# Up projection as a seven-product Strassen scheme, with separate up and down phases, in a two-layer streaming encoder

## The chip, the cores and the metric

The kernel runs on one core of a Trainium2 chip. The metric is the device time of one execution in microseconds (us), as the median of several runs. The engines are called PE (matrix products; PEld is its weight load), DVE (elementwise work on vectors), ACT (functions, scaled copies, casts), POOL (small general work) and SP (a queue that issues transfers, DMA). PSUM is the memory that PE accumulates into: 8 banks of 128 partitions by 512 numbers. SBUF is the memory that all engines work from. DRAM is outside both.

## The reference, cut to what matters

Two layers, each over 1024 rows of one prompt stream and 8 x 16 rows of running streams, 1152 rows in all (9 tiles of 128 rows):

```python
def conv_ffn(x, prev, w_up, conv_w, conv_b, w_down):
    h = x @ w_up                                   # 1024 -> 2 * 2816
    l = h.shape[1]
    full = pad_or_concat(prev, h)                  # two earlier rows in front
    c = conv_b
    for j in range(CONV_W):                        # CONV_W = 3
        c = c + full[:, j:j + l] * conv_w[j]
    gate, val = jnp.split(c, 2, axis=-1)
    y = (jax.nn.silu(gate) * val) @ w_down         # 2816 -> 1024
    return y, full[:, -(CONV_W - 1):]

def trunk_layer(x, ...):
    xn = rms_norm(x, norm_mix)
    q, k, v, u = mixer_inputs(xn, ...)             # one projection, 1024 -> 1280
    x = x + concat([attention(q, k, v), pool_mixer(u, ...)]) @ w_out
    f, new_conv = conv_ffn(rms_norm(x, norm_ffn), conv_prev, w_up, conv_w, conv_b, w_down)
    return x + f, ...
```

Everything is float32. The two products of the feed-forward part, with `w_up` and with `w_down`, are most of the arithmetic.

## The kernel before, in words

A float32 product is made of three matmuls on numbers split into a high and a low part (`mm3`, L157 to L160: high by high on L158, high by low on L159, low by high on L160). A split is a cast to the shorter type for the high part, and a subtraction for the low part. For weights ACT makes the high part and DVE the low part (`w_split`; L188 and L189 without a norm gain, L198 and L199 where the gain of the norm in front is multiplied in, one instruction for each 128 rows of the weight). A weight piece is 128 x 512 numbers, 256 KB; it goes through one of five `raw` buffers. The queue of SP issues all transfers.

Each layer has a first half (norm, input projection, pooling, attention, output projection) and a feed-forward half. In the first half the units of work carry a key from a table (`PLAN`), and `arrange` sorts them by key within limits on buffers. All units then stand in one list; the language's scheduler sets each engine's final order from it.

The feed-forward half goes over 22 column tiles i of 128 gate columns and 128 value columns. For each, `up_units` makes two pieces of weight (four blocks of 128 rows each) for the gate and two for the value, and multiplies them with the normed, transposed and split rows in three blocks of 384: 2 x 3 blocks x 8 k x 3 = 144 matmuls of 384 columns. `up_evac` copies a finished block out of PSUM (L783), convolves it (L800 on ACT, two L802 on DVE), applies SiLU on ACT (L812), multiplies gate and value (L817) and splits the result (L822 on ACT, L823 on DVE). After every second i, `down_units` multiplies the two gated tiles with their rows of `w_down`: nine row tiles, two halves of 512 output columns, 12 matmuls of 512 columns for a row tile, and adds each half into the resident rows (L868, `X`, nine tiles of 128 x 1024 kept in SBUF through the whole kernel). So up and down work alternate on PE, and the down work of the last pair of layer 0 is carried into the first half of layer 1.

PSUM has three tags: `mm` with four banks (projections, up), `s` and `tr` with two each (attention, transposes, down). Norms: ACT squares and sums a row tile (L245), POOL takes the power, and ACT (L249) or DVE (L251) scales it; PE transposes it (L267), ACT and DVE split it (L270, L271).

Of the kernel before, what the change touches and what calls it, by code (L numbers as in the profile page):

```python
# [19 lines left out]
C_ID, C_M, C_COS, C_SIN, C_RC, C_END = 0, 128, 384, 456, 528, 592  # L20

# [20 lines left out]
def arrange(tokens, limits):  # L42
    """Orders tokens by key, holding each back until its predecessors and its buffers are there."""
# [17 lines left out]
# priorities of the first half of a layer: stream -> (first, step), attention: start of each tile  # L61
# [19 lines left out]
def encoder_kernel(ctx: ExitStack, tc: tile.TileContext, consts, x_prompt, x_sample, cache_k, cache_v,  # L81
# [6 lines left out]
    def mkpool(name, bufs, space=None):  # L88
# [5 lines left out]
    ps = mkpool("ps", 1, bass.MemoryType.PSUM)  # L94

    BUFS = dict(T6=12, G=3, raw=5, w=8, S=2, K=2, PT=4, Q=4, u=2, sA=1, sB=1, D=2, V=5, qkv=4, xn=2,
                st=15, ks=1)
    SIZE = dict(T6=1536, G=1536, raw=512, w=512, S=1024, K=1024, PT=512, Q=512, u=520, sA=520, sB=520, D=384,
                V=128, qkv=640, xn=1024, st=16, ks=512)
# [15 lines left out]

    def P(tag):
        cnt[0] += 1
        return ps.tile([128, 512], F32, tag=tag, name=f"{tag}{cnt[0]}", bufs={"mm": 4, "s": 2, "tr": 2}[tag])
# [12 lines left out]
    gcol = cp.tile([128, 2, 2, 8], F32, name="gcol")  # L131
# [4 lines left out]
    X = [cp.tile([128, DM], F32, name=f"x{t}") for t in range(NT)]  # L136

    state = {}
    defer = []
# [23 lines left out]
    order = []  # L163
    wptr = {"dma": 0, "split": 0}

    def w_dma(w):
        w.raw = sp.tile([128, SIZE["raw"]], F32, tag="raw", name=f"raw{cnt[0]}", bufs=BUFS["raw"])
        cnt[0] += 1
        w.raw = w.raw[:, 0:w.n]
        w.load(w.raw)  # L170

    def w_split(w):
        if not w.split:
            return
        if w.dst is None:
            if w.wide:
                g = T("G", [128, 2, 512], F32R)
                w.hi, w.lo = g[:, 0], g[:, 1]
            else:
                w.hi = T("w", [128, w.n], F32R)  # L180
                w.lo = T("w", [128, w.n], F32R)
        else:
            w.hi, w.lo = w.dst()
        if w.gain is None:
            if w.dve:
                dve.tensor_copy(out=w.hi, in_=w.raw)
            else:
                act.copy(out=w.hi, in_=w.raw)  # L188
            dve.tensor_tensor(out=w.lo, in0=w.raw, in1=f32(w.hi), op=ALU.subtract)  # L189
        else:  # L190
            kn = w.gain.shape[1]
            raw, hi, lo = [v.rearrange("p (k n) -> p k n", k=kn) for v in (w.raw, w.hi, w.lo)]
            for k in range(kn):
                g = w.gain[:, k:k + 1]
                if w.dve:
                    dve.tensor_scalar(out=hi[:, k], in0=raw[:, k], scalar1=g, scalar2=None, op0=ALU.mult)
                else:
                    act.mul(out=hi[:, k], in_=raw[:, k], mul=g)  # L198
                dve.scalar_tensor_tensor(out=lo[:, k], in0=raw[:, k], scalar=g, in1=f32(hi[:, k]), op0=ALU.mult, op1=ALU.subtract)  # L199
        w.raw = None  # L200

    def w_advance(pos):
        upto, more = pos + 1, 0
        while upto < len(order) and more < min(order[pos].ahead, order[upto].ahead):
            more += order[upto].dst is None and order[upto].split
            upto += 1
# [539 lines left out]
    def up_units(l, i, val, first):  # L746
# [6 lines left out]
        def mms(w, p, bs):  # L753
            wh, wl = [v.rearrange("p (k n) -> p k n", k=4) for v in (w.hi, w.lo)]
            for b in bs:
                if p == 0:
                    hold[b] = P("mm")
# [402 lines left out]
```

## Time and profile before

| what | value |
|---|---|
| median of three runs | 2372.83 us (2372.5 to 2374.82) |
| span of the profiled execution | 2370.1 us |
| PE busy, share of the span | 2337.6 us, 99% |
| DVE busy | 1486.5 us, 63% |
| ACT busy | 1179.9 us, 50% |
| feed-forward half of layer 0, about | 348 to 1178 us |
| feed-forward half of layer 1, about | 1536.9 to 2365.9 us |
| moved by DMA, mean rate | 146.95 MB, 62 GB/s |

The profiled execution has a time of its own, its span; 2.7 us lie between the span and the median. In the rows quoted below a group has its line, engine, operation, the program's names, the shape (partitions x columns), the count, then the busy time in us, the mean of one in ns, and the idle time of the engine ahead of them. Windows list the length of the stretch, then for PE, PEld, DVE, ACT and POOL the busy time and the number of instructions, the granted clock of PE (1.00 is full), the share of DMA and its rate in GB/s. A timeline row has start, duration, engine, and the instruction. A matmul's duration there contains its fill and drain: what one matmul costs in a stream is the distance from its start to the next start.

### The profile page before, as it was taken

To read this page: it belongs to the slowest core of one execution; us is meant where nothing else is said; L and a number is where in the kernel's file an instruction comes from. 1 tells how busy PE (TensorE), PEld (TensorE's weight loads), DVE (VectorE), ACT (ScalarE), POOL (GpSimd) and SP (SyncE) were. 2 spreads that over 40 slices of the span, in tenths; PEclk is the share of its full clock that TensorE was granted. 3 is DMA by queue.
4 is the path that set the end of the run, shared out by engine and by line. 5 is a ranking of instruction groups with operands and counts; after the bars stand their busy time and mean duration, and the time that the engine had idled before them with its cause. 6 is when DMAs were issued, how large, how long until landed. Compare 5 with 4: busy or idle time off the path is not lost.

```text
span 2370.1 us, 35379 instructions
## 1 busy us (share of the span) xinstructions
PE 2337.6 (99%) x12555; PEld 2118.1 (89%) x12555; DVE 1486.5 (63%) x3508; ACT 1179.9 (50%) x2889; POOL 153.1 (6%) x499
## 2 busy tenths in 40 slices
PE   7999999999999999999999999999999999999999
PEld 6878679999999999999988887899999999999998
DVE  5887756656555566555677867565556655565555
ACT  5766656335433354434557666564345433453332
POOL 0010000000000000000000100000000000000000
PEclk9999999999999999999999999999999999999999
DMA  7332232101111111111133323211111111111102
GB/s 231 98 96 84 74 89 68 46 28 55 45 46 42 32 55 45 42 45 33 46 94 89 90 84 93 83 59 46 42 32 55 45 42 40 38 54 41 46 27 82
DMA packets 166403, 146.95 MB, mean 62 GB/s; under 512 B 13522, under 2 KB 133826, under 8 KB 166194
## 3 DMA queue, kind: packets, MB, share of 16 engines
q1 hardware_dynamic: 166226, 144.70, 20.4%
q8 instruction: 98, 1.61, 0.3%
q14 instruction: 79, 0.65, 0.1%
HBM read 137.91 MB, written 8.44 MB: 62 GB/s over the span
## 4 chain that ended last, share of the span: by engine, by line
PE 96%; DMA 1%; DVE 1%; ACT 1%; issue 0%; SPq 0%; POOL 0%; ACTq 0%; DVEq 0%
PE mm L158 21%; PE mm L160 21%; PE mm L159 21%; PE s L158 4%; PE tr L158 4%; PE tr L159 4%; PE s L159 4%; PE tr L160 4%; PE s L160 4%; PE s L574 2%; PE tr L267 1%; DMA raw<-in_w_in_dram 1%; PE tr L561 1%; PE mm L390 1%; PE tr L497 1%; PE s L522 1%
## 5 line engine op out<-in xcount | busy, mean ns | idle before, releaser
L158 PE MATMUL mm<-T,w 128*128 128x384 f32 x2252 | 755.4, 336 | 1.0 <-ACT u L339 1.0
L159 PE MATMUL mm<-T,w 128*128 128x384 f32 x2252 | 754.2, 335 | 0.1
L160 PE MATMUL mm<-T,w 128*128 128x384 f32 x2252 | 753.8, 335 | 0.0
L158 PEld LDWEIGHTS mm<-T,w 128*128 128x128 f32 x2252 | 422.9, 188 | 5.7 <-ACT u L339 1.4
L159 PEld LDWEIGHTS mm<-T,w 128*128 128x128 f32 x2252 | 422.9, 188 | 4.5 <-DVE T L271 0.4
L160 PEld LDWEIGHTS mm<-T,w 128*128 128x128 f32 x2252 | 422.8, 188 | 2.7
L198 ACT ACTIVATE w<-raw,gcol 128x128 fp32r<-128x128 f32 (+2 forms) x854 | 313.1, 423 | 131.6 <-PE mm L159 116.0
L199 DVE SCALAR_TENSOR_TENSOR w<-raw,gcol,w 128x128 fp32r<-128x128 f32 (+2 forms) x854 | 292.3, 384 | 128.1 <-ACT w L198 126.7
L868 DVE TENSOR_TENSOR x<-tr,x 128x512 f32<-128x512 f32 x198 | 136.5, 690 | 200.9 <-PE tr L160 200.7
L188 ACT CAST S<-raw 128x512 fp32r<-128x512 f32 x44 | 25.3, 619 | 475.6 <-PE tr L159 475.6
L802 DVE SCALAR_TENSOR_TENSOR u<-PT,cvp,u 128x384 f32<-128x384 f32 (+1 forms) x256 | 159.2, 622 | 100.7 <-ACT u L800 97.7
L868 DVE TENSOR_TENSOR x<-s,x 128x512 f32<-128x512 f32 x198 | 136.6, 690 | 108.4 <-PE s L160 108.3
L159 PE MATMUL mm<-w,T 128*128 128x512 f32 (+1 forms) x504 | 191.2, 380 | 0.1
L160 PE MATMUL mm<-w,T 128*128 128x512 f32 (+1 forms) x504 | 189.4, 377 | 0.5 <-DVE T L271 0.5
L158 PE MATMUL mm<-w,T 128*128 128x512 f32 (+1 forms) x504 | 176.1, 388 | 5.1 <-ACT w L198 4.8
L783 ACT COPY PT<-mm 128x384 f32<-128x384 f32 x176 | 84.7, 481 | 163.2 <-PE mm L160 163.2
L802 DVE SCALAR_TENSOR_TENSOR sB<-PT,cvp,sB 128x384 f32<-128x384 f32 (+1 forms) x130 | 80.5, 620 | 72.0 <-ACT sB L800 69.5
L802 DVE SCALAR_TENSOR_TENSOR sA<-PT,cvp,sA 128x384 f32<-128x384 f32 (+1 forms) x142 | 88.5, 623 | 54.4 <-ACT sA L800 50.6
L158 PEld LDWEIGHTS mm<-w,T 128*128 128x128 f32 x504 | 95.0, 193 | 22.2 <-ACT w L198 5.6
L780 POOL COPY PT<-PT 128x2 f32<-128x2 f32 x176 | 33.1, 189 | 1264.4 <-issue 1092.4
L822 ACT CAST G<-Q 128x384 fp32r<-128x384 f32 x132 | 67.8, 514 | 93.3 <-DVE Q L817 92.8
L160 PEld LDWEIGHTS mm<-w,T 128*128 128x128 f32 x504 | 96.6, 192 | 18.8 <-DVE T L271 2.4
(219 smaller groups left out, 3857.2 us busy)
## 6 DMA issues: line engine op xcount, KB each, us to landing
raw<-in_w_up_dram SPq DMA_DIRECT2D x176, 256.0 KB
raw<-in_w_in_dram SPq DMA_DIRECT2D x120, 256.0 KB
raw<-in_w_down_dram SPq DMA_DIRECT2D x88, 256.0 KB
raw<-in_w_out_dram SPq DMA_DIRECT2D x48, 256.0 KB
raw<-in_w_out_dram SPq DMA_DIRECT2D x96, 128.0 KB
out_dram<-x SPq DMA_DIRECT2D x9, 512.0 KB
x<-in_x_prompt_dram SPq DMA_DIRECT2D x8, 512.0 KB
out_dram<-V SPq DMA_DIRECT2D x104, 8.0 KB
```

What stands on the lines that cost most here:

```text
L158: pe.matmul(out=out, lhsT=a[0], rhs=b[0], start=first, stop=False)
L159: pe.matmul(out=out, lhsT=a[0], rhs=b[1], start=False, stop=False)
L160: pe.matmul(out=out, lhsT=a[1], rhs=b[0], start=False, stop=last)
L188: act.copy(out=w.hi, in_=w.raw)
L198: act.mul(out=hi[:, k], in_=raw[:, k], mul=g)
L199: dve.scalar_tensor_tensor(out=lo[:, k], in0=raw[:, k], scalar=g, in1=f32(hi[:, k]), op0=ALU.mult, op1=ALU.subtract)
L574: pe.matmul(out=o, lhsT=V, rhs=H.pop(("p", g, kk)), start=kk == kks[0], stop=kk == 1)
L780: pool.tensor_copy(out=hb[:, 0:2], in_=state["hb", val, b - 1][:, 384:386])
L783: act.copy(out=hb[:, 2:386], in_=p[:, 0:384])
L802: dve.scalar_tensor_tensor(out=c, in0=hb[:, j:j + W], scalar=cvp[:, j, ct:ct + 1], in1=c, op0=ALU.mult, op1=ALU.add)
L822: act.copy(out=g[:, f], in_=sg)
L868: dve.tensor_tensor(out=xs, in0=o, in1=xs, op=ALU.add)
```

## The change

The change replaces the up projection's plain product by a scheme of seven products. The inner dimension is cut into two halves of 512, the rows into halves (each 576-row group s into two parts of 288, `QT`), and the gate and value columns of tile i are the two column blocks. From the four blocks of rows three sums and one more are made, and from the four weight blocks four more combinations; seven products of a weight combination and a row combination are taken (`PRODUCTS`), and gate and value follow from them by additions.

- The rows: `normQ` transposes the normed rows into quarters `F`; `sums(s)` makes, for each of two groups, four sums and seven splits of 128 x 1152. The norm's gain is multiplied into the rows in `normA`, so weight splits carry no gain.
- The weights: `up_load` issues the four pieces of tile i, `up_prep` makes four combinations `T1` to `T4` and seven splits, four products ahead (`LAG`).
- The products: 7 products x 2 groups x 4 k x 3 = 168 matmuls of 288 columns for a tile i. They go to banks 0 to 5 of PSUM, two banks for a product, in turn over three pairs. PSUM is now one tile whose banks are handed out by hand.
- `up_post` recombines: product 0 is copied by ACT, the others are added by DVE. `conv` and `gate` then work on 1168 columns at once, and the gated rows go to DRAM (`gd`).
- The down projection is a phase of its own after all 22 tiles, in three chunks of 8, 8 and 6 tiles of `gd`. A chunk's rows of `w_down` are split once and stay in SBUF; for each of nine row tiles `down_load` brings the gated rows (512-byte runs) and the residual rows, and the sum goes back to DRAM (`xd`). The residual rows are no longer resident. The last chunk of layer 0 (nine units of 36 matmuls) is what is carried into the first half of layer 1.

```diff
     def normA(l, t, which):
...
+            dve.scalar_tensor_tensor(out=xn, in0=X, scalar=s[:, 2:3], in1=state["gb", which], op0=ALU.mult, op1=ALU.mult)
...
+    def sums(s):
...
+        def split(name, q, h, last):
+            def f():
+                src = F(q, h)
+                hi = T("B", [128, 4, QT], F32R)
+                lo = T("B", [128, 4, QT], F32R)
+                act.copy(out=hi, in_=src)
+                dve.tensor_tensor(out=lo, in0=src, in1=f32(hi), op=ALU.subtract)
...
+        return [split("A11", *x11, False), split("A12", *x12, False), split("A22", *x22, False),
+                add(x22, x21, x22, ALU.add), split("S1", *x22, False),
+                add(x21, x11, x21, ALU.subtract), add(x11, x22, x11, ALU.subtract), split("S2", *x11, False),
+                split("S3", *x21, True), add(x12, x12, x11, ALU.subtract), split("S4", *x12, True),
...
+    PRODUCTS = (("B11", "A11"), ("B21", "A12"), ("T2", "S2"), ("T1", "S1"), ("T3", "S3"), ("B22", "S4"), ("T4", "A22"))
+    def up_prep(l, j):
+        i, n = divmod(j, 7)
...
+        if n == 2:
+            make("T3", "B22", "B12", ALU.subtract)
+            make("T2", "T3", "B11", ALU.add)
+            make("T1", "B12", "B11", ALU.subtract)
+            make("T4", "B21", "T2", ALU.subtract)
...
+        act.copy(out=hi, in_=src)
+        dve.tensor_tensor(out=lo, in0=src, in1=f32(hi), op=ALU.subtract)
...
+    def up_mm(l, i, n, ss):
+        name, a = PRODUCTS[n]
+        pair = (7 * i + n) % 3
+        hi, lo = state["upw", 7 * i + n]
+        for s in ss:
+            ah, al = state["A", s, a]
+            o = psum[:, 2 * pair + s, 0:QT]
+            for k in range(4):
+                c = slice(k * 128, (k + 1) * 128)
+                mm3(o, (hi[:, c], lo[:, c]), (ah[:, k], al[:, k]), k == 0, k == 3)
...
+    def up_post(l, i, n, ss):
...
+        if n == 0:
+            for o, y in zip(xf, uf):
+                act.copy(out=o, in_=y)
+        elif n == 1:
+            add(hb_first(row(0), ss), uf, xf)
+        elif n == 2:
+            add(xf, uf, xf)
+        elif n == 3:
+            add(rows_first(sum_("tot"), ss), uf, xf)
+        elif n == 4:
+            add(xf, uf, xf)
+            add(hb_second(row(1), ss), us, rows_second(sum_("tot"), ss))
+        elif n == 5:
+            add(hb_first(row(1), ss), uf, rows_first(sum_("tot"), ss))
...
+                conv(l, i, 1)
+        elif n == 6:
+            add(hb_second(row(0), ss), us, rows_second(x, ss))
...
+                later(1, lambda: gate(l, i))
...
+    def conv(l, i, val):
...
+        act.activation(out=c, in_=h[:, 2:1170], func=AF.Identity, scale=cvp[:, 2, ct:ct + 1], bias=cvp[:, 3, ct:ct + 1])
+        for j in (1, 0):
+            dve.scalar_tensor_tensor(out=c, in0=h[:, j:j + 1168], scalar=cvp[:, j, ct:ct + 1], in1=c, op0=ALU.mult, op1=ALU.add)
...
+    def down_load(l, c, t):
+        a, e = CHUNKS[c]
...
+        sync.dma_start(out=f32(lo).rearrange("p (f n) -> p f n", n=128),
+                       in_=gd[l][a:e, :, t * 128:(t + 1) * 128].rearrange("f p n -> p f n"))
+        act.copy(out=hi, in_=f32(lo))
+        dve.tensor_tensor(out=lo, in0=f32(lo), in1=f32(hi), op=ALU.subtract)
+        X = T("B", [128, DM])
+        sync.dma_start(out=X, in_=xd[c][t])
...
+    def down_units(l, after):
...
+                if x + 1 < len(seq):
+                    down_load(l, *seq[x + 1])
...
+                    for ff in range(a, e):
+                        w = state["wd", ff]
+                        g = [v[:, (ff - a) * 128:(ff - a + 1) * 128] for v in (hi, lo)]
+                        mm3(o, g, [v[:, hs] for v in w], ff == a, ff == e - 1)
+                        if h == 1 and t == NT - 1:
...
+                                down_prep(l, e + ff - a)
+                    dve.tensor_tensor(out=X[:, hs], in0=o, in1=X[:, hs], op=ALU.add)
...
-        ff, pend = ffn(l, after)
-        events += ff
+        events += up_units(l)
+        down = down_units(l, after)
+        pend = down[-NT:]
+        events += down[:-NT]
```

**How the engines' orders change.** In the rows below a name with a number is a buffer: `raw` an unsplit weight piece, `Q` a combination of two pieces, `W`, `u`, `sA`, `sB` a split weight, `psum` the products, `PT` their partial sums, `B` a large buffer (rows, sums, split rows, gated rows). Rows that only repeat the kind of one shown are left out. DVE in the middle of the feed-forward half, one column tile before:

```order
L868 TENSOR_TENSOR x_80<-tr_6477,x_80 128x512
L189 TENSOR_TENSOR S_6488<-raw_6190,S_6487 128x512
L189 TENSOR_TENSOR K_6625<-raw_6485,K_6624 128x512
L199 SCALAR_TENSOR_TENSOR w_6631<-raw_6491,gcol,w_6630 128x128 x4
L802 SCALAR_TENSOR_TENSOR sB_6573<-PT_6570,cvp,sB_6573 128x384 x2
L817 TENSOR_TENSOR Q_6280<-sB_6573,Q_6280 128x384
L823 TENSOR_TENSOR G_6578<-Q_6280,G_6578 128x384
```

And now, from the addition after product 5 of a tile to the gate:

```order
L943 TENSOR_TENSOR B_8601<-psum,PT_8571 128x2x288
L869 TENSOR_TENSOR u_8730<-raw_8470,u_8729 128x512
L943 TENSOR_TENSOR B_8502<-psum,PT_8464 128x288
L992 SCALAR_TENSOR_TENSOR B_8646<-B_8601,cvp,B_8646 128x1168
L943 TENSOR_TENSOR B_8502<-psum,PT_8464 128x160
L943 TENSOR_TENSOR B_8502<-psum,PT_8464 128x8x16
L869 TENSOR_TENSOR sB_8760<-Q_8611,sA_8759 128x512
L851 TENSOR_TENSOR Q_8855<-raw_8723,Q_8851 128x512
L992 SCALAR_TENSOR_TENSOR B_8684<-B_8502,cvp,B_8684 128x1168
L869 TENSOR_TENSOR W_8788<-raw_8721,W_8788 128x512
L943 TENSOR_TENSOR B_8757<-psum,PT_8719 128x2x288
L999 TENSOR_TENSOR B_8601<-B_8684,B_8646 128x1024
```

What moved: the adds into the rows (L868) and the splits of `w_down` are gone from the loop, and DVE, which did not read the up product's PSUM before, now frees each pair of banks itself. The second place is DVE where the first half of a layer ends. Before, the last transposed rows are split in small pieces among other work:

```order
L271 TENSOR_TENSOR T_4193<-tr_4215,T_4191 128x4x128
L802 SCALAR_TENSOR_TENSOR sA_4403<-PT_4400,cvp,sA_4403 128x384
L271 TENSOR_TENSOR T_4192<-tr_4222,T_4190 128x4x128
L189 TENSOR_TENSOR K_4507<-raw_4328,K_4506 128x512
L817 TENSOR_TENSOR Q_4305<-sA_4403,Q_4305 128x384
```

And now (L326 is a split of `sums`, L334 one of its additions, L869 and L851 the weights of the first tiles):

```order
L869 TENSOR_TENSOR W_4130<-raw_4108,W_4130 128x512
L334 TENSOR_TENSOR B_3903<-B_3896,B_3903 128x1152
L334 TENSOR_TENSOR B_3896<-B_3504,B_3896 128x1152
L326 TENSOR_TENSOR B_3939<-B_3903,B_3938 128x1152
L334 TENSOR_TENSOR B_3504<-B_3903,B_3504 128x1152
L326 TENSOR_TENSOR B_3945<-B_3504,B_3944 128x1152
L326 TENSOR_TENSOR B_3954<-B_3511,B_3953 128x1152
L943 TENSOR_TENSOR B_3986<-psum,PT_3969 128x288 x2
```

The sums of a whole group now stand in one run ahead of the first addition from PSUM. The third place has no counterpart before: SP where the up products end and the down phase begins.

```order
L1044 DMA raw_10017<-in_w_down_dram 128x512
L1044 DMA raw_10030<-in_w_down_dram 128x512
L1053 DMA B_9485<-gd_78 128x8x128
L1013 DMA out_dram<-V_9609 2x128
L1058 DMA B_9490<-xd_74 128x1024
L1053 DMA B_9492<-gd_78 128x8x128
L1002 DMA gd_78<-B_9409 128x1152
```

The first gated rows (L1053) are asked for behind loads of `w_down` that wait for a free `raw` buffer, and the store of the last gated tile (L1002) stands behind the second request.

More of the change, by code (lines that the diff above doesn't have):

```diff
@@ L174, in w_split @@
             return
[L175 to L181, printed above, removed]
-        else:
[L183 to L199, printed above, removed]
+        g = T("B" if w.wide else "W", [128, 2, 512], F32R)
+        w.hi, w.lo = g[:, 0, 0:w.n], g[:, 1, 0:w.n]
+        if w.dve:
+            dve.tensor_copy(out=w.hi, in_=w.raw)
+        else:
+            act.copy(out=w.hi, in_=w.raw)
+        dve.tensor_tensor(out=w.lo, in0=w.raw, in1=f32(w.hi), op=ALU.subtract)
         w.raw = None
@@ L204, in w_advance @@
         while upto < len(order) and more < min(order[pos].ahead, order[upto].ahead):
-            more += order[upto].dst is None and order[upto].split
+            if order[upto].layer != order[pos].layer:
+                break
+            more += order[upto].split
             upto += 1
         while wptr["split"] < min(upto, len(order)):
-            while wptr["dma"] < min(wptr["split"] + 5, len(order)):
+            while wptr["dma"] < min(wptr["split"] + 5, len(order)) and order[wptr["dma"]].layer == order[pos].layer:
                 w_dma(order[wptr["dma"]])
@@ L212, in w_advance, with w_first @@
             wptr["split"] += 1
+    def w_first(l):
+        for _ in range(3):
+            w_dma(order[wptr["dma"]])
+            wptr["dma"] += 1
     def run(u):
@@ L262, in f @@
             xn = state.pop(("xn", t))
+            for i, (a, e) in enumerate(KG):
+                tr = P("tr")
+                for k in range(a, e):
+                    pe.transpose(out=tr[:, (k - a) * 128:(k - a + 1) * 128], in_=xn[:, k * 128:(k + 1) * 128], identity=ident)
+                tv = tr[:, 0:(e - a) * 128].rearrange("p (k n) -> p k n", n=128)
+                hi, lo = [xT[j][i][:, 0:e - a, tl * 128:(tl + 1) * 128] for j in range(2)]
+                act.copy(out=hi, in_=tv)
+                dve.tensor_tensor(out=lo, in0=tv, in1=f32(hi), op=ALU.subtract)
@@ new lines, in down_prep @@
+    def down_prep(l, f):
+        hi, lo = [T("B", [128, DM], F32R) for _ in range(2)]
+        for h in range(2):
+            r = raw_tile()
+            c = slice(h * 512, (h + 1) * 512)
+            sync.dma_start(out=r, in_=w_down[l][f * 128:(f + 1) * 128, c])
+            act.copy(out=hi[:, c], in_=r)
+            dve.tensor_tensor(out=lo[:, c], in0=r, in1=f32(hi[:, c]), op=ALU.subtract)
+        state["wd", f] = hi, lo
+    def down_load(l, c, t):
+        a, e = CHUNKS[c]
+        n = (e - a) * 128
+        lo, hi = [T("B", [128, n], F32R) for _ in range(2)]
+        sync.dma_start(out=f32(lo).rearrange("p (f n) -> p f n", n=128),
[4 more added lines that the diff above has]
+        sync.dma_start(out=X, in_=xd[c][t])
+        state["g", c, t] = hi, lo, X
```

576 lines of the change are left out of this document (322 added, 254 removed).

## The prediction

> **What bounds the kernel now.** I read the page's first part and its chain, then windows by stage, then the groups by shape, then single starts in the timeline. First the busy times, the rate in 40 slices, and the chain that ended last by engine:
>
> ```profile
> PE 2337.6 (99%) x12555; PEld 2118.1 (89%) x12555; DVE 1486.5 (63%) x3508; ACT 1179.9 (50%) x2889; POOL 153.1 (6%) x499
> ...
> GB/s 231 98 96 84 74 89 68 46 28 55 45 46 42 32 55 45 42 45 33 46 94 89 90 84 93 83 59 46 42 32 55 45 42 40 38 54 41 46 27 82
> ...
> PE 96%; DMA 1%; DVE 1%; ACT 1%; issue 0%; SPq 0%; POOL 0%; ACTq 0%; DVEq 0%
> ```
>
> PE is the chain. By stage (first halves of both layers, then their feed-forward halves):
>
> ```profile
> 0.00:348.00 348.00, 326.67 (x1775) 269.82 (x1776) 246.82 (x728) 221.17 (x550) 29.60 (x30) 0.97 0.36 110
> 348.00:1178.00 830.00, 829.65 (x4443) 778.92 (x4442) 494.02 (x1031) 372.37 (x902) 48.68 (x224) 1.00 0.16 46
> 1178.00:1536.90 358.90, 352.47 (x1926) 291.85 (x1926) 254.79 (x736) 228.42 (x565) 27.40 (x23) 0.98 0.30 87
> 1536.90:2365.90 829.00, 828.79 (x4416) 777.52 (x4414) 490.20 (x1016) 357.95 (x872) 47.38 (x222) 1.00 0.15 46
> ```
>
> In the feed-forward halves PE never waits and its clock is full: 0.35 and 0.21 us idle in 830 and 829. There the time is a count of matmuls by what one costs, and only fewer or cheaper matmuls make it shorter. DVE has work for 59% of it (490.20 of 829.00). The price of a matmul is the distance of starts:
>
> ```profile
> 911.99 0.33 PE L158 MATMUL mm<-T,w 128*128 128x384 f32 x1
> ...
> 913.90 0.34 PE L160 MATMUL mm<-T,w 128*128 128x384 f32 x1
> ...
> 49.43 0.28 PE L158 MATMUL mm<-G,T 128*128 128x256 f32 x1
> ...
> 50.39 0.28 PE L159 MATMUL mm<-G,T 128*128 128x256 f32 x1
> ...
> 900.13 0.39 PE L159 MATMUL tr<-K,G 128*128 128x512 f32 x1
> ...
> 903.10 0.39 PE L160 MATMUL tr<-K,G 128*128 128x512 f32 x1
> ```
>
> Eleven steps of 384 columns take 1.91 us, 0.1736 each; eight of 256 take 0.96, 0.120 each; thirteen of 512 take 2.97, 0.2285 each. So a column costs 0.42 ns and a matmul about 13 ns besides, and 288 columns come by interpolation to 0.120 + 32/128 x 0.0536 = 0.1334 us. Check: a layer's up and down matmuls, 22 x 144 = 3168 at 0.1736 and 22 x 54 = 1188 at 0.2285, make 550 + 271 = 821 of the 829 us.
>
> **Term 1, the up products: -114 us.** Before, 6336 x 0.1736 = 1100 us. Now 2 x 22 x 168 = 7392 x 0.1334 = 986 us. The seven products save an eighth of the columns, and the shorter matmuls give back 1056 x 13 ns = 14 us of it. For a column tile i: 168 x 0.1334 = 22.4 us against 144 x 0.1736 = 25.0. The down matmuls are as many as before, 2376.
>
> The Trainium skill ("TensorE: Matmul & The Clock Gate", "Back-to-back issue gap") gives N/2.4 + 2.5 ns for a full clock. That would be 162.5 and 122.5 ns, and -124 us for this term; the trace has 173.6 where the rule has 162.5, so I keep the rows.
>
> This term holds only where PE stays the bound in the loop. **DVE in the loop.** Its prices, by shape, and two instructions of 512 columns run back to back:
>
> ```profile
> L189 DVE TENSOR_TENSOR w<-raw,w 128x512 fp32r<-128x512 f32 x88 | 60.1, 685 | 26.3 <-ACT w L188 23.1 <-PE tr L624 2.5 <-PE mm L158 0.4
> L443 DVE TENSOR_TENSOR qkv<-qkv,st 128x640 f32<-128x640 f32 x18 | 14.7, 818 | 0.3 <-POOL st L437 0.3
> L802 DVE SCALAR_TENSOR_TENSOR u<-PT,cvp,u 128x384 f32<-128x384 f32 x172 | 106.3, 618 | 97.4 <-ACT u L800 95.2
> ...
> 911.47 1.29 DVE L189 TENSOR_TENSOR K<-raw,K 128x512 fp32r<-128x512 f32 x2
> ```
>
> A column costs (818 - 685)/128 = 1.04 ns, and of two in a row the second adds 1.29 - 0.685 = 0.605 us, 80 ns less than one alone. So by estimate 288 columns cost 0.37, 576 0.67, 1024 1.14, 1152 1.27, and a convolution step of 1168 618 + 784 x 1.04 - 80 = 1.35 us. For a column tile: eleven of 512 (seven splits, four combinations) 6.7; five additions of 576 3.4; six of the second parts (288, 160 and 128, twice) 1.6; four convolution steps 5.4; the gate 1.3. Sum 18.4 of 22.4 us: PE is still the longer. What can hold PE inside a tile is a pair of banks not yet freed: the pair of product n is written again by product n+3, so its reader has two products, 6.4 us. The tightest is the addition after product 1 of the next tile, which in DVE's order stands behind product 6's additions, three splits, one combination and four convolution steps (about 8.7 us after product 6 ends). Product 4, which needs its banks, begins 12.8 us after. Four us are spare, so I cost waits in the loop at +5 us in all (0 to 1.1 us for each of 44 tiles; the upper end is the second rival).
>
> ACT has, for a tile, seven casts, one copy, two passes of 1168 and one SiLU:
>
> ```profile
> L188 ACT CAST w<-raw 128x512 fp32r<-128x512 f32 x88 | 53.7, 621 | 36.0 <-PE mm L159 23.0 <-DMA raw<-in_w_out_dram 12.1 <-DVE G L199 0.6
> L249 ACT ACTIVATE xn<-x,st 128x1024 f32<-128x1024 f32 x10 | 11.5, 1160 | 0.4 <-POOL st L247 0.4
> ```
>
> That is 7 x 0.62 + 0.7 + 3 x 1.3 = 9 us, far from the bound. Weights: four pieces of 256 KB a tile. Five such loads, and the rate while they landed:
>
> ```profile
> 910.38 3.82 SPq L237 DMA_DIRECT2D raw<-in_w_up_dram  x5
> ...
> 912.00:917.00 5.00, 5.00 (x30) 5.00 (x30) 3.63 (x9) 2.57 (x7) 0.54 (x4) 1.00 0.87 247
> ```
>
> At 247 GB/s 1.05 MB take 4.2 us, in a tile of 22.4. They can be issued only when the combinations have left their buffers (five of `raw`), about 5 us after product 6; they land at about 12, when the first combination of the next tile is due in DVE's order with some 3.5 us to spare.
>
> **Term 2, the sums at the end of the first half: +30 us.** From the first residual addition of the last output projection to the last split of the second group, and on to the recombination of the first tile, DVE has 22 instructions of 1152 (27.9 us), 33 of 512 (20.0), three of the norm (3.6) and about 5 of small ones and additions: 56 us. PE has there 57 matmuls of 512 (13.0), 168 of 288 (22.4), and transposes (about 5.6): 41 us. Second-group products wait for the sums, and DVE's order has these ahead of the first addition from PSUM, so I take the whole difference, 15 us, for each of two layers. Bounds: nothing, if enough of it runs earlier beside attention; 25 a layer, if PE also stands while three pairs of banks wait for that first addition.
>
> **Term 3, from up to down: +18 us.** After the last product: its additions (0.8), one ACT pass (1.3) and the rest of the convolutions on DVE, four of 1.35, and then the split of the first gated rows: its low part is there at about 7.5 us. The gated rows themselves are asked for behind five loads of `w_down` (SP's rows shown above), which land at 4.2 us for a megabyte; I put them at 5 and their high part at 6.1. PE so stands about 6.4 us. A pause has a second price here, the clock. At the start, and in layer 1's attention:
>
> ```profile
> 33.00:36.00 3.00, 0.38 (x4) 0.18 (x2) 0.00 (x0) 0.00 (x0) 0.00 (x0) 0.89 0.51 196
> 36.00:39.00 3.00, 0.83 (x4) 0.83 (x5) 0.85 (x3) 1.39 (x4) 0.00 (x0) 0.50 0.53 182
> 39.00:42.00 3.00, 3.00 (x16) 3.00 (x16) 2.43 (x7) 1.91 (x5) 0.00 (x0) 0.50 0.69 188
> 42.00:45.00 3.00, 3.00 (x24) 3.00 (x24) 2.26 (x6) 2.76 (x7) 0.00 (x0) 0.97 0.66 208
> ```
>
> PE was hardly busy for some 5 us (0.38 and 0.83 of 6.00), and then 3 us at full load ran at half clock, with 16 matmuls where the next 3 us hold 24. So a pause of this length costs 2 to 3 us more: 9 us in a layer, bounds 4 and 14.
>
> **Term 4, inside the down phase: +6 us.** A row tile of 48 matmuls lasts 48 x 0.2285 = 11.0 us and moves 0.52 MB of gated rows, 0.52 in and 0.52 out of residual rows: 143 GB/s, under the 247 seen for runs of the same 512 bytes. At two changes of chunk in a layer the next `w_down` rows must be split: 0 to 3 us each, 1.5 taken.
>
> **Term 5, the first halves: +5 us.** The gain arrives by a broadcast load, the norm's scaling moves to DVE, casts of weights become cheaper (one instruction of 512 for four of 128), banks are handed out by hand, and more down work (nine units of 36 matmuls, not 12) lies in layer 1's first half, where PE idles 358.90 - 352.47 = 6.4 us. No row prices the new order; bounds -15 and +20.
>
> Sum on the span: 2370.1 - 114 + 5 + 30 + 18 + 6 + 5 = 2320; the 2.7 us outside it added: **2323 us**, 2.1% faster.
>
> **Rivals.** *The transitions are hidden.* If terms 2 and 3 cost a quarter, since the sums run beside attention, where DVE was busy for 254.79 of 358.90 us, and ACT and DVE reach the first down rows in time: 2323 - 36 = 2287. Against it stands DVE's order, with sums in a run. 0.17.
>
> *The recombination becomes the bound of the loop.* One mechanism: DVE, in order, waits for two ACT passes (1.3 each) between an addition and its convolution, and for late weight pieces ahead of the first combination (3.2): 18.4 + 2.6 + 3.2 = 24.2 us a tile, 44 x 1.8 = +79, or 2323 - 5 + 79 = 2397, slower. For it: DVE goes from 59% to 82% in the loop, and its idle ahead of L802 is mostly put down to ACT (95.2 of 97.4). It decides from 22.4 + (2373 - 2318)/44 = 23.6 us a tile. 0.12.
>
> *The down phase is bound by transfers.* At the 98 GB/s of the second slice a row tile would take 16 us; 36 such tiles x 5 = +180, near 2500. It decides below 143 GB/s. Against it: 247 in the row above. 0.05.
>
> *A matmul of 288 columns costs as much as one of 384,* since its weight load sets the pace: 7392 x 0.1736 = 1283, +183 where I have -114, so 2620. The row of 256 columns, each with a load of its own, at 0.120 speaks against it. 0.02.
>
> The Trainium skill (the same section) also gives a sustained 81 ns at 128 columns and 131 ns at 512, where columns count for little: by a line between these 288 would cost 102 and 384 114 ns, and the term would be 754 - 724 = +30 us. The 0.2285 measured at 512 is against it, so the rival keeps its 0.02.
>
> *The change doesn't do what it says* has no chance of its own: the orders show seven products a tile.
>
> **How the numbers follow.** The forecast has 0.64, the rivals 0.17, 0.12, 0.05 and 0.02. Its own range from the bounds: terms 2 to 5 between about -20 and -40 on the one side, and +45 on the other: 2283 to 2368. The range to 2376 takes in the lower part of the second rival, and 2278 most of the first. Under 0.2% (5 us) no change could be told: faster is 0.61 + 0.17 + a part of the second rival under 23.5 us a tile, 0.03; same 0.04; slower 0.15.
>
> **What would show it.** Term 1: rows of 288 columns start 0.133 us apart, and a tile lasts 22.4 us in windows of the up phase with PE over 98%. Term 2: windows at the layer's middle with DVE full and PE short by some 15 us. Term 3: a PE gap of 5 to 8 us behind the last product, with the clock at half after it. Term 4: a row tile each 11.0 us. I am wrong if PE has gaps in every tile, if the 288-column step is over 0.15 us, or if the rate in the down phase falls under 143 GB/s.

## The result: slower, by what is lost outside the changed products

The changed kernel takes 2414.97 us (median of four runs, 2412.21 to 2419.12) against 2372.66 for the kernel before beside it: a ratio of 1.0178, 95% interval 1.0164 to 1.0193. Forecast were 2323 us and a range of 2278 to 2376. Its profiled execution has a span of 2410.8 us. The first part of its page, the rate in 40 slices, and the chain by engine:

```profile
PE 2280.5 (95%) x13610; PEld 2025.8 (84%) x13610; DVE 1596.4 (66%) x2942; ACT 959.7 (40%) x1774; POOL 201.6 (8%) x411
...
GB/s 218 62 112 122 99 117 89 84 79 70 79 75 71 77 75 225 131 218 164 143 135 61 99 127 102 133 89 65 65 80 78 69 79 75 79 246 125 222 157 109
...
PE 82%; DVE 7%; DMA 5%; ACT 3%; issue 2%; SPq 1%; POOL 0%; ACTq 0%; DVEq 0%
```

PE is busy for less time than before and the span is longer, so PE waits: 2410.8 - 2280.5 = 130.3 us where it was 32.5. The view of the cores gives the mean granted clock, before and then after:

```profile
core 0: 2370.1 us, clock 0.991
```

```profile
core 0: 2410.8 us, clock 0.969
```

What the clock takes is (1 - 0.991) x 2370.1 = 21 us before and 0.031 x 2410.8 = 75 after. These two sums count the half clock also while PE stands idle; laid over PE's busy time alone, the trace's record of the clock takes 18 us before and 57 after. So the balance of the spans, +40.7 us, reads: the up products -114 (as forecast), waits +98, clock while PE works +39, and 18 that I leave unexplained. Where the waits lie, from windows of the changed kernel (first half, up phase, the passage, chunks 0 and 1 of the down phase; then the same for layer 1, whose first half holds chunk 2 of layer 0, and whose down phase has three chunks):

```profile
0.00:450.00 450.00, 386.77 (x2006) 312.54 (x2006) 296.27 (x750) 237.89 (x570) 34.51 (x36) 0.92 0.37 117
450.00:931.40 481.40, 479.94 (x3612) 479.35 (x3612) 414.43 (x617) 194.46 (x257) 67.64 (x172) 1.00 0.25 80
931.40:937.00 5.60, 0.06 (x2) 0.03 (x1) 5.05 (x5) 2.08 (x4) 0.00 (x0) 0.80 0.88 276
937.00:1135.00 198.00, 198.00 (x845) 160.13 (x846) 64.32 (x83) 37.35 (x51) 0.00 (x0) 0.99 0.55 179
1135.00:1640.00 505.00, 457.95 (x2349) 370.22 (x2348) 309.64 (x761) 248.53 (x582) 32.42 (x31) 0.94 0.36 113
1640.00:2121.00 481.00, 479.22 (x3613) 478.70 (x3611) 414.50 (x612) 193.03 (x256) 66.69 (x170) 1.00 0.25 80
2121.00:2127.60 6.60, 0.43 (x3) 0.11 (x1) 6.51 (x8) 3.82 (x4) 0.39 (x2) 0.88 0.80 236
2127.60:2410.80 283.20, 278.15 (x1188) 224.67 (x1188) 85.65 (x112) 42.49 (x55) 0.00 (x0) 0.99 0.51 166
```

The up phase, 481 us in each layer, is as full as the feed-forward half was before: 479.94 of 481.40, at full clock. The loss is in the first halves and their ends: 63.2 and 47.1 us without work on PE, and by the clock column 0.08 x 450 = 36 and 0.06 x 505 = 30 us more. Before it was 21.3 and 6.4 us idle, and 0.03 x 348 = 10 and 0.02 x 359 = 7 by the clock. The difference is some 131 us, where the forecast had 35 (terms 2 and 5). With the clock counted over busy time alone it is some 116.

Two stretches stand out. From the first attention products to a third of them, and from the last attention product into the up phase, each for both layers (after):

```profile
78.00:170.00 92.00, 78.13 (x396) 61.14 (x396) 64.96 (x213) 50.85 (x135) 6.83 (x4) 0.91 0.30 93
1274.00:1369.00 95.00, 84.13 (x436) 66.37 (x437) 64.83 (x209) 54.14 (x141) 6.45 (x4) 0.95 0.26 79
334.00:460.00 126.00, 100.49 (x558) 80.64 (x557) 86.58 (x136) 62.39 (x126) 11.20 (x15) 0.82 0.31 92
1520.00:1660.00 140.00, 110.33 (x620) 89.72 (x619) 94.78 (x146) 67.73 (x133) 11.19 (x21) 0.83 0.27 83
400.00:450.00 50.00, 40.62 (x229) 35.07 (x227) 48.05 (x55) 29.67 (x48) 5.84 (x7) 0.81 0.31 93
```

The same stretches before:

```profile
81.00:175.00 94.00, 93.70 (x512) 78.72 (x510) 79.21 (x248) 64.71 (x165) 8.49 (x5) 1.00 0.36 106
1255.00:1348.00 93.00, 92.92 (x508) 78.17 (x507) 76.71 (x241) 65.84 (x168) 7.56 (x5) 1.00 0.37 108
299.00:400.00 101.00, 100.97 (x600) 87.59 (x599) 60.61 (x137) 61.03 (x145) 6.79 (x18) 0.95 0.29 83
1472.00:1600.00 128.00, 127.89 (x750) 113.73 (x749) 76.85 (x173) 77.14 (x184) 9.04 (x28) 0.96 0.25 73
```

In the first pair DVE and ACT are less busy than before and PE waits 14 and 11 us: no engine is the bound there. In the last stretch of the second group, 400 to 450 us, DVE is full (48.05 of 50) and PE has 40.62. So there are two different troubles, and the theories for the experiments are these. **O**, the order: banks handed out by hand are reserved in the arrangement of the first half, which moves projections apart that ran interleaved. **N**, the norm with its gain on DVE. **X**, residual rows fetched ahead of weights. **R**, raw buffers blocked (found after the first four runs). **T**, DVE as the bound where the row sums are made.

### The profile page after: what moved, and what is told of

Its sections match the earlier page's. It is cut to its first block, busy times and chain, and to the rows that moved or that the text cites. A ratio compares the mean times of both kernels' runs of the same rounds, so it can differ in the third digit from the quotient of the medians.

```text
span 2410.8 us, 35976 instructions
## 1 busy us (share of the span) xinstructions
PE 2280.5 (95%) x13610; PEld 2025.8 (84%) x13610; DVE 1596.4 (66%) x2942; ACT 959.7 (40%) x1774; POOL 201.6 (8%) x411
## 4 chain that ended last, share of the span: by engine, by line
PE 82%; DVE 7%; DMA 5%; ACT 3%; issue 2%; SPq 1%; POOL 0%; ACTq 0%; DVEq 0%
PE psum L173 25%; PE psum L174 25%; PE psum L175 25%; PE psum L658 2%; DMA raw<-in_w_out_dram 2%; DVE W L199 1%; PE psum L305 1%; DVE B L326 1%; DMA raw<-in_w_in_dram 1%; PE psum L645 1%; DMA B<-gd 1%; DMA raw<-in_w_down_dram 1%; DVE B L334 1%; PE psum L461 1%; ACT W L198 1%
## 5 line engine op out<-in xcount | busy, mean ns | idle before, releaser
L173 PE MATMUL psum<-B,W 128*128 128x288 f32 (+1 forms) x1896 | 572.2, 302 | 18.3 <-ACT B L325 12.3
L174 PE MATMUL psum<-B,W 128*128 128x288 f32 (+1 forms) x1896 | 569.9, 301 | 8.1 <-DVE B L326 8.1
L175 PE MATMUL psum<-B,W 128*128 128x288 f32 (+1 forms) x1896 | 568.2, 300 | 0.0
L173 PEld LDWEIGHTS psum<-B,W 128*128 128x128 f32 x1896 | 359.4, 190 | 22.6 <-ACT B L325 13.9
L173 PE MATMUL psum<-B,B 128*128 128x512 f32 (+2 forms) x914 | 357.0, 394 | 20.1 <-ACT B L1055 10.3
L174 PEld LDWEIGHTS psum<-B,W 128*128 128x128 f32 x1896 | 358.8, 189 | 11.2 <-DVE B L326 10.2
L175 PEld LDWEIGHTS psum<-B,W 128*128 128x128 f32 x1896 | 358.9, 189 | 0.9 <-DVE W L199 0.5
L174 PE MATMUL psum<-B,B 128*128 128x512 f32 (+2 forms) x914 | 357.2, 391 | 0.0
L175 PE MATMUL psum<-B,B 128*128 128x512 f32 (+2 forms) x914 | 355.9, 391 | 0.0
L992 DVE SCALAR_TENSOR_TENSOR B<-B,cvp,B 128x1168 f32<-128x1168 f32 x176 | 250.5, 1428 | 7.9 <-ACT B L990 7.7
L173 PEld LDWEIGHTS psum<-B,B 128*128 128x128 f32 x914 | 172.9, 190 | 59.8 <-ACT B L198 11.5
L174 PEld LDWEIGHTS psum<-B,B 128*128 128x128 f32 x914 | 173.5, 190 | 37.6 <-DVE B L199 0.5
L175 PEld LDWEIGHTS psum<-B,B 128*128 128x128 f32 x914 | 172.8, 189 | 37.7 <-issue 0.2
L173 PE MATMUL psum<-W,B 128*128 128x512 f32 (+1 forms) x510 | 190.4, 386 | 9.5 <-ACT B L463 5.0
L199 DVE TENSOR_TENSOR W<-raw,W 128x512 fp32r<-128x512 f32 x184 | 125.8, 689 | 103.4 <-ACT W L198 102.7
L174 PE MATMUL psum<-W,B 128*128 128x512 f32 (+1 forms) x510 | 192.9, 379 | 0.9 <-DVE W L199 0.9
L868 ACT CAST W<-Q 128x512 fp32r<-128x512 f32 x132 | 81.8, 621 | 280.3 <-PE psum L175 280.1
L175 PE MATMUL psum<-W,B 128*128 128x512 f32 (+1 forms) x510 | 191.9, 381 | 0.0
L198 ACT CAST W<-raw 128x512 fp32r<-128x512 f32 x184 | 113.2, 620 | 166.9 <-PE psum L175 58.5
L943 DVE TENSOR_TENSOR B<-psum,PT 128x160 f32<-128x160 f32 (+2 forms) x356 | 147.8, 447 | 27.2 <-PE psum L175 27.1
L943 DVE TENSOR_TENSOR PT<-psum,PT 128x576 f32<-128x576 f32 (+1 forms) x138 | 100.4, 730 | 84.6 <-PE psum L175 84.3
```

The source lines that it names most:

```text
L173: pe.matmul(out=out, lhsT=a[0], rhs=b[0], start=first, stop=False)
L174: pe.matmul(out=out, lhsT=a[0], rhs=b[1], start=False, stop=False)
L175: pe.matmul(out=out, lhsT=a[1], rhs=b[0], start=False, stop=last)
L868: act.copy(out=hi, in_=src)
L943: dve.tensor_tensor(out=o, in0=x, in1=y, op=ALU.add)
L992: dve.scalar_tensor_tensor(out=c, in0=h[:, j:j + 1168], scalar=cvp[:, j, ct:ct + 1], in1=c, op0=ALU.mult, op1=ALU.add)
```

## The experiments

**The order alone, in the kernel before.**

```diff
-            kres = {7: {"qkv": 3}, 11: {"V": 3}}
+            kres = {0: {"mm": 3}, 7: {"qkv": 3, "mm": -3}, 8: {"mm": 3}, 11: {"V": 3, "mm": -3}}
...
-            stream(f"o{b}", ou, pre, {15: {"T6": -4}})
+            stream(f"o{b}", ou, pre, {0: {"mm": 3}, 7: {"mm": -3}, 8: {"mm": 3}, 15: {"T6": -4, "mm": -3}})
...
-        ev = arrange(toks, {"T6": 12, "qkv": 4, "V": BUFS["V"], "xn": 1})
+        ev = arrange(toks, {"T6": 12, "qkv": 4, "V": BUFS["V"], "xn": 1, "mm": 4})
```

(and two banks for a column pair of the pooling projection, `u`)

> The kernel before, with one thing of the change: the projections reserve their PSUM banks in the arrangement of the first half (three of four for a block of the input or output projection, two for the pooling projection), so that an output projection and a pooling projection no longer run interleaved. Nothing else moves. Theory O (the order): the 92 us that the first halves lost in the changed kernel come from this rearrangement, so this kernel takes 2372.7 + 50 to 90 = 2423 to 2463 us. Theory N (the norm: DVE scales with the gain, which is first fetched) and theory X (residual rows fetched from DRAM ahead of weights): this kernel stays within 10 us of 2372.7.

Measured: 2421.03 us, ratio 1.0204 (1.0188 to 1.0219), +49 us, just under the interval that theory O gave. The order costs a kernel some 2% in which nothing else is changed. Its loss is at the end of the attention and at the end of the first half, not between 81 and 177 us:

```profile
81.00:177.00 96.00, 94.14 (x505) 78.05 (x504) 78.64 (x241) 64.98 (x165) 8.96 (x5) 1.00 0.34 103
249.00:306.00 57.00, 47.15 (x209) 35.49 (x208) 35.62 (x124) 33.18 (x91) 4.63 (x4) 0.85 0.22 66
306.00:400.00 94.00, 85.22 (x446) 67.50 (x445) 48.11 (x107) 44.72 (x106) 5.31 (x8) 0.84 0.25 74
```

PE waits 9.9 and 8.8 us there, and by the clock column 9 and 15 us more are lost (0.15 x 57 and 0.16 x 94); the kernel before loses about 5 by the clock between 299 and 400 us too.

**One bank for the pooling projection, in the changed kernel.**

```diff
-                us.append(Unit(f, [in_piece(w_in[l], 2 * j, 768 + c * 256)]))
+                us.append(Unit(f, [in_piece(w_in[l], 4 * (j % 2), 768 + c * 256 + j // 2 * 128, 4, 128)]))
...
-{0: {"mm": 2}, 3: {"mm": -2}, 4: {"mm": 2}, 7: {"T6": -6, "mm": -2}}
+{0: {"mm": 1}, 1: {"mm": -1}, 2: {"mm": 1}, 3: {"mm": -1}, 4: {"mm": 1}, 5: {"mm": -1}, 6: {"mm": 1}, 7: {"T6": -6, "mm": -1}}
```

> The changed kernel, but the pooling projection's weights come in pieces of four k by 128 columns in place of two k by 256, so that it needs one bank at a time; with it the arranged order of the first half is nearly that of before again. As many matmuls, as many bytes. Theory O: 2415 - 50 to 80 = 2335 to 2365 us. Theories N and X: 2405 to 2420 us.

Measured: 2412.45 us, 1.0170 (1.0153 to 1.0187). Not to be told from the changed kernel: theory O failed here. Something else held PE in the same places, it seems, and the second and third output projection were still apart (three banks each, four there are), which this edit doesn't change.

**Without the gain.**

```diff
-            dve.scalar_tensor_tensor(out=xn, in0=X, scalar=s[:, 2:3], in1=state["gb", which], op0=ALU.mult, op1=ALU.mult)
+            if t < 3:
+                act.mul(out=xn, in_=X, mul=s[:, 2:3])
+            else:
+                dve.tensor_scalar(out=xn, in0=X, scalar1=s[:, 2:3], scalar2=None, op0=ALU.mult)
```

(the gain's load is left out too, so this kernel leaves the gain out of the computation)

> The changed kernel without the norm gains: they are left out of the computation altogether (no broadcast load, and the norm scales as in the kernel before, three row tiles on ACT and six on DVE). Theory N: the gain's cost is the loss of the first halves, 2415 - 30 to 80 = 2335 to 2385 us. Theories O and X: within 12 us of 2415, since DVE saves 36 x 0.45 = 16 us spread over both first halves, most of it not on the path.

Measured: 2407.32 us, 1.0148 (1.0133 to 1.0163), 8 us less. Theory N is worth some 8 us and isn't the cause.

**Residual rows one by one.**

```diff
-                    if c == 0 and j == 0:
-                        x_load(l, range(3 * b, 3 * b + 3))()
+                    if c == 0 and j in (1, 3, 5):
+                        x_load(l, [3 * b + j // 2])()
```

> The changed kernel, with the residual rows of an output projection's three row tiles (three loads of 512 KB) asked for one by one at its units 1, 3 and 5 in place of all at unit 0, so that no 1.5 MB stand ahead of weight pieces in SP's queue. Theory X: six such bursts of about 6 us, 2415 - 20 to 40 = 2375 to 2395 us. Theories O and N: within 8 us of 2415.

Measured: 2402.20 us, 1.0126 (1.0111 to 1.0141), 13 us less: below what X gave, above the rest. That a load of 1.5 MB in front of weights is felt at all says that the weights arrive just in time, which led to the raw buffers.

The view of the line that casts weight pieces (L198) in the changed kernel, 60 to 180 us, has the small pieces (`W`), those for a large buffer (`B`), and for what ACT sat idle ahead of them (us, times):

```profile
L198 ACT CAST W<-raw x15: 608/620/625, 64.0 to 179.4; 128x512 fp32r<-128x512 f32 x15
L198 ACT CAST B<-raw x12: 600/626/632, 77.6 to 176.2; 128x512 fp32r<-128x512 f32 x12
...
  DMA raw<-in_w_out_dram: 12.6, 9
  DMA raw<-in_w_in_dram: 8.9, 4
```

ACT waits 21.5 us for weights to land; before, in the same stretch, such a wait is 2.2 us. I then followed each weight piece in the trace from the issue of its load to the start of its cast. In layer 0, 16 pieces that are split into a large buffer (three of seven in one part of the first half) stay 18.2 us in their raw buffer on average, one 49.5; the rest 9.2. Before, such pieces had three buffers of their own and stayed 4.7 us, the rest 11.9. Now they share the 33 large buffers with the rows and sums. From 105 to 160 us two or three of the five raw buffers are held in this way, and the small pieces are cast 2.7 to 4.0 us after the issue of their loads, as soon as they land. That became theory R.

**No piece in a large buffer.**

```diff
-            w.wide = i % 7 in (2, 4, 6)
-            w.ahead = LA
+            w.wide = False
```

> The changed kernel, but no weight piece of the first half is split into a large buffer any more (three of seven were, each from one of the 33 large buffers that the rows now share); all go through the five small ones, split at most two pieces ahead in place of four. Theory R (raw): in the changed kernel a piece meant for a large buffer waits in its raw buffer, 18 us on average where the other pieces need 9, so that only one or two of the five raw buffers turn and each piece is loaded just in time; without such pieces the first halves lose 25 to 50 us less: 2365 to 2390 us. Theory O (the order alone): 2410 to 2425 us, since the order of the work is untouched and the pieces have fewer buffers. Theory X: 2405 to 2420 us.

Measured: 2388.37 us, 1.0064 (1.0049 to 1.0079), 27 us less, as R gave and neither O nor X. The edit also lets these pieces be split only two ahead in place of four; that part wasn't run alone. And at the place that R names:

```profile
78.00:168.00 90.00, 84.05 (x450) 68.94 (x449) 64.76 (x207) 54.48 (x139) 6.43 (x4) 0.96 0.32 102
1260.00:1359.00 99.00, 94.23 (x497) 77.31 (x498) 75.48 (x232) 61.23 (x152) 6.43 (x4) 0.97 0.31 95
322.00:460.00 138.00, 113.38 (x649) 93.58 (x648) 97.61 (x151) 69.48 (x134) 17.17 (x21) 0.84 0.27 86
1494.00:1660.00 166.00, 136.44 (x818) 115.61 (x817) 118.37 (x180) 78.58 (x147) 14.41 (x29) 0.86 0.27 84
```

PE's wait in the first pair fell from 13.9 and 10.9 us to 6.0 and 4.8; the ends of the first halves wait as long as they did, 24.6 and 29.6 us.

**Three repairs together**, that is no piece in a large buffer, one bank for the pooling projection, residual rows one by one; no new edit.

> The changed kernel with three edits together: no piece in a large buffer, the pooling projection with one bank at a time, and the residual rows asked for one by one. Theories R and O together: the order of before pays only where the weights are there in time, so here it does: 2415 - 13 (residual rows) - 25 to 50 (raw) - 20 to 40 (order) = 2312 to 2357 us. Theory R without O: 2352 to 2377 us. If neither holds, 2400 us as with the residual rows alone.

Measured: 2390.57 us, 1.0075 (1.0058 to 1.0092). Not to be told from the last run, and outside both intervals: a miss for both theories. The residual rows' 13 us, it seems, are no longer there to be had once raw buffers turn, and the order, half restored, gave nothing a second time.

**Six raw buffers.**

```diff
-    BUFS = dict(B=33, W=5, raw=5, ...)
+    BUFS = dict(B=33, W=5, raw=6, ...)
...
-            while wptr["dma"] < min(wptr["split"] + 5, len(order)) ...
+            while wptr["dma"] < min(wptr["split"] + 6, len(order)) ...
```

> The last kernel with six raw buffers and weights asked for six pieces ahead in place of five. Theory R: what is left of the first halves' loss is still partly the loading of pieces just in time, so 5 to 20 us less than the last kernel. If no raw buffer is short any more, within 4 us of it.

Measured: 2384.66 us, 1.0048 (1.0033 to 1.0063), 6 us less, at the low end of what R gave and little more than the noise. Raw buffers are nearly enough now: with this and the next edit ACT waits 0.7 us for weights between 60 and 180 us, where it waited 21.5.

**The whole order of before.**

```diff
-                            hold[tl] = mm_take()
+                            hold[tl] = mm_take() if (b, c) != (2, 0) or tl == 0 else turn["s"][tl - 1]
...
+            m = 1 if b == 2 else 3
-            stream(f"o{b}", ou, pre, {0: {"mm": 3}, 7: {"mm": -3}, 8: {"mm": 3}, 15: {"T6": -6, "mm": -3}})
+            stream(f"o{b}", ou, pre, {0: {"mm": m}, 7: {"mm": -m}, 8: {"mm": 3}, 15: {"T6": -6, "mm": -3}})
```

(the two banks of the scores are not given back as projection banks, and the projection that borrows them waits for the last step of the attention)

> The last combination (no piece in a large buffer, one bank for the pooling projection, residual rows one by one, six raw buffers), and the first half of the last output projection takes two of its three banks from the scores, which are done by then. With this the arranged order of each first half is that of the kernel before, row for row. Theory O: the kernel before lost 49 us when this order was taken from it, a third of it at the end of the first half, so 2385 - 20 to 45 = 2340 to 2365 us. Theory T (at the end of the first half DVE is the bound, whatever the order of PE's work): within 8 us of 2385.

Measured: 2371.72 us, 0.9995 (0.9985 to 1.0004): 13 us less, and level with the kernel before. The half of the order that mattered here is the overlap of the last two output projections, which this edit restores; the waits at the ends of the first halves fell from 24.6 and 29.6 us (without pieces in large buffers) to 17.5 and 20.7. The gain is less than O gave, and T's "within 8 us" failed as well. What is left of the ends of the first halves:

```profile
319.00:450.00 131.00, 113.55 (x649) 94.24 (x648) 94.38 (x145) 67.75 (x130) 11.29 (x21) 0.86 0.33 106
1490.00:1620.00 130.00, 109.33 (x619) 89.96 (x618) 90.40 (x137) 64.78 (x125) 10.73 (x19) 0.86 0.32 103
```

17.5 and 20.7 us of waits, and by the clock column 0.14 x 131 = 18 us in each.

**Without the additions of the row sums.**

```diff
         def add(o, a, b, op):
             def f():
-                dve.tensor_tensor(out=F(*o), in0=F(*a), in1=F(*b), op=op)
+                pass
```

> The changed kernel without the eight additions of 128 x 1152 that make the row sums of a layer; they are left out of the computation, the seven splits stay. DVE has 8 x 1.27 = 10 us less to do at the end of each first half. Theory T: PE's loss there (25 us idle and 22 us of half clock in a layer) shrinks by about as much and takes half clock with it, 2415 - 20 to 40 = 2375 to 2395 us. Theories O and R: within 8 us of 2415.

Measured: 2392.29 us, 1.0075 (1.0059 to 1.0092), 23 us less than the changed kernel for 10.8 us less of work on DVE in each layer (eight of 1.352). The two stretches, 125 and 150 us long, now wait 19.1 and 20.4 us:

```profile
335.00:460.00 125.00, 105.87 (x611) 84.88 (x610) 83.12 (x137) 66.19 (x131) 12.65 (x19) 0.86 0.30 90
1510.00:1660.00 150.00, 129.61 (x767) 109.91 (x766) 101.40 (x164) 76.00 (x143) 13.35 (x27) 0.85 0.29 89
```

What DVE is spared there, the kernel is spared: T holds for this place, in the kernel without the repairs. Leaving an addition out also leaves out that the splits wait for it, so the run doesn't separate DVE's load from the length of the chain.

**The additions on POOL** (on the kernel with the order of before; `pool.tensor_tensor` in place of `dve.tensor_tensor`).

> The first kernel of this call with the eight additions of a layer's row sums on POOL, which is idle there, in place of DVE. Theory T: 10 to 30 us under the first kernel. If POOL's additions are so slow, or so much in DVE's way, that the splits behind them come later still: 0 to 15 us over it.

Measured: 2391.83 us, 1.0080 (1.0061 to 1.0099), 20 us slower than with them on DVE, outside both intervals. The row points to the cause:

```profile
L334 POOL TENSOR_TENSOR B<-B,B 128x1152 f32<-128x1152 f32 x16 | 50.0, 3125 | 27.6 <-DVE B L326 17.7 <-PE psum L175 9.0
```

3.1 us each where DVE needs 1.35, in a chain that splits on DVE wait for and that itself waits for them.

**The first gated rows earlier.**

```diff
+                        if n == 4:
+                            down_load(l, 0, 0)
...
-                if x == 0:
-                    down_load(l, c, t)
```

> The kernel with the order of before and the four repairs, and the first gated and residual rows of the down phase asked for and split two products ahead of the end of the up phase (after product 4 of the last column tile), as soon as the large buffers are free. Theory of term 3: PE stands some 5 us at that place and loses 2 to 3 more to the clock, in each layer; with the rows there it stands under 1.5 us: 2372 - 10 to 18 = 2354 to 2362 us. If the wait is for the last convolutions in DVE's queue and not for the rows, within 5 us of 2372.

Measured: 2366.95 us, 0.9975 (0.9965 to 0.9985): 5 us under the kernel without it, half of what term 3's theory gave and by the number within what the other one gave, and faster than both kernels of the case by a little. The trace speaks for the rows all the same: PE's idle time at the passage fell from 4.9 and 5.5 us to 3.3 and 2.9, and what is left is a wait for the cast of these rows, not for convolutions. The clock column is 0.83 over the 20 us around each passage (905 to 925, 2075 to 2095; without the edit the same). ACT waits for the load:

```profile
904.79 0.38 SPq L1056 DMA_DIRECT2D B<-gd  x1
...
911.20 1.04 ACT L1058 CAST B<-B 128x1024 fp32r<-128x1024 f32 x1 [5.39 <-DMA B<-gd]
```

The load was issued only some 4 us before the last product ended, in SP's order behind loads of `w_down`, and needed 6.4 us to land beside them.

**The weight combinations on POOL** for the first three tiles of a layer, on top of that.

```diff
-            dve.tensor_tensor(out=w(name), in0=w(a), in1=w(b), op=op)
+            (pool if i < 3 else dve).tensor_tensor(out=w(name), in0=w(a), in1=w(b), op=op)
```

> The last kernel with the four weight combinations of the first three column tiles of a layer on POOL in place of DVE. Theory T: DVE has 12 x 0.6 = 7 us less at the end of each first half, 5 to 20 us under the last kernel. The additions on POOL took 3.1 us each and made the kernel 20 us slower, since splits waited for them; the combinations are due later, but if POOL's chain of three is again what the splits wait for, 0 to 10 us over the last kernel.

Measured: 2371.94 us, 0.9996 (0.9988 to 1.0005), 5 us over the last. A combination takes 1.3 to 2.4 us on POOL where DVE needs 0.69, and ACT's casts wait 8.4 us in all for combinations; that this eats the gain on DVE is likely, not shown.

## Why the prediction was wrong, step by step

**Term 1 held.** A matmul of 288 columns, in the up phase of the changed kernel:

```profile
699.94 0.29 PE L173 MATMUL psum<-B,u 128*128 128x288 f32 x1
...
701.54 0.30 PE L173 MATMUL psum<-B,u 128*128 128x288 f32 x1
```

Twelve steps take 1.60 us, 0.1333 each against 0.1334 forecast. The fourth rival is out, and with it the sustained figures of the Trainium skill ("TensorE: Matmul & The Clock Gate", "Back-to-back issue gap"); its isolated rule, 122.5 ns, is as much too low here as it was at 384 columns.

**The loop held.** PE waits 1.5 and 1.8 us in the two up phases, where I had put 5 in all. DVE is busy for 414.43 of 481.40 us, 86%, forecast 82%: a convolution step took 1.43 us where the estimate had 1.35. The second rival is out.

**Term 3 held, term 4 has none of its pauses.** PE stands 5.5 us at the passage of layer 0 and 6.2 in layer 1 (forecast 6.4), with half clock behind it:

```profile
934.00:937.00 3.00, 0.03 (x1) 0.03 (x1) 2.45 (x3) 1.12 (x2) 0.00 (x0) 0.62 0.92 297
937.00:940.00 3.00, 3.00 (x7) 2.42 (x8) 2.52 (x3) 1.77 (x2) 0.00 (x0) 0.50 0.97 293
```

The down phase then runs without a gap, 198.00 of 198.00 us busy with a change of chunk in it, at 179 GB/s: the third rival is out, and the pauses that term 4 priced are not there. Its matmuls came out a little dearer instead: 845 in 198.00 us and 1188 in 278.15 are 0.234 us each where the forecast had 0.2285, some 12 us in all, of which the clock of 0.99 takes about 5.

**Term 2 failed as a size, by the clock.** In the run with the order of before, term 2 begins at the first residual addition of the last output projection, at about 375 and 1550 us. The stretches above, cut there:

```profile
319.00:375.00 56.00, 49.41 (x259) 36.62 (x258) 26.38 (x56) 26.05 (x69) 2.76 (x5) 0.82 0.38 123
375.00:450.00 75.00, 64.14 (x392) 57.62 (x391) 68.00 (x89) 41.71 (x63) 8.53 (x16) 0.89 0.30 93
1490.00:1550.00 60.00, 51.45 (x265) 38.34 (x264) 27.13 (x54) 27.74 (x69) 2.37 (x5) 0.83 0.36 116
1550.00:1620.00 70.00, 57.88 (x355) 51.63 (x355) 63.27 (x84) 37.05 (x57) 8.36 (x14) 0.88 0.29 92
```

From there on PE waits 10.9 and 12.1 us: "I take the whole difference, 15 us, for each of two layers" was a little too much. But I priced the clock behind a pause in term 3 and not in term 2, where the pauses are several and short. By the column it takes 0.11 x 75 = 8 and 0.12 x 70 = 8 us more. So this term is some 40 us and not 30; in the changed kernel itself, cut likewise at 385 and 1575 us, it is some 53.

Ahead of the sums, beside the running streams' attention, PE waits 6.6 and 8.6 us, and the clock takes 10 in each. This is not term 2, and only half of that clock is new. The kernel before in the same work, and a part of it:

```profile
299.00:348.00 49.00, 48.97 (x281) 38.94 (x280) 26.97 (x61) 27.74 (x65) 3.38 (x5) 0.90 0.26 72
1472.00:1536.90 64.90, 64.90 (x370) 51.97 (x369) 35.23 (x78) 35.20 (x84) 3.38 (x5) 0.92 0.29 86
332.00:343.00 11.00, 11.00 (x52) 8.57 (x53) 1.90 (x7) 3.52 (x10) 0.44 (x1) 0.53 0.01 1
```

PE never waits there, and the clock takes 5 us in each. The last row is near half clock with PE busy throughout, more than half of it with matmuls of 64 columns.

**Term 5 failed as a step.** "+5, bounds -15 and +20" treated the first half as the same work with other prices. It wasn't: its buffers were taken away. The 33 large buffers serve rows, split rows, sums and weight pieces at once, where weight pieces had three of their own; the banks are reserved by hand; residual rows come from DRAM. In the changed kernel the first halves lose 131 us more than before, 53 of them at the sums, so term 5 is some 78 and not 5. The repairs show 27 us for the first, 13 for the order on top of it, 6 for a sixth raw buffer, 13 for the residual rows where nothing else is repaired. Together they bring 43 of the 92 us that lie between forecast and result. The front part of the document lists the banks and the residual rows, and I had looked for their price in durations, where they have none; that the weight pieces lose their buffers I had not listed.

**What stays open.** The kernel with the order of before is still 49 us above the forecast. About 10 of that is term 2, and some 42 is term 5: 25 just ahead of the sums, as told, and 22 in the rest of the first halves, where PE waits 30.6 and 19.3 us and waited 21.3 and 6.4, less the 5 that were forecast. These parts are read from windows and count some clock in idle time, so they don't add up to the microsecond. The longest waits there are for the norm's scaling (11.1 us on L269 in layer 0) and for the attention's scaling and copies on DVE and ACT, hardly for weights (1.9 us in layer 0); why they are longer than before was not tried. Nor was it tried whether all the waits at the sums are DVE's. And no run here holds the clock up without taking the pauses away, so the clock's share is read from its column and isn't tested by itself.

## What to carry to other kernels

A change that needs room takes it from somebody: list for every buffer tag and bank that disappears or is merged who used it, and ask which queue stops when its holder waits. Here a piece that waits in a staging buffer stopped the loads behind it, 27 us that no instruction's duration shows. And where pauses on PE are forecast, price the clock behind them each time, short ones too: at the sums, in the kernel with the order of before, 23 us of pauses went with 17 us by the clock column. Then compare with the kernel before at the same work, which can lose some of it already.

## What the runs showed of the hardware that I had not expected

POOL needs 3.1 us for an addition of 128 x 1152 that DVE does in 1.35, and 1.3 to 2.4 us for one of 128 x 512 (DVE 0.69), so that an idle POOL was no relief for a chain that others wait for. The clock falls in more places than behind the one pause that I had looked at: between 334 and 460 us the changed kernel has no pause over 5 us and a mean clock of 0.82, and between 332 and 343 us the kernel before has no pause at all and a clock of 0.53.
